# Rotating 96 images by 180 degrees: the innermost piece of the first group is turned ahead of the last quarter of the second group

## Chip, core and metric

The kernel runs on one core of a Trainium2 chip. The metric is the device time in microseconds (us) of one execution. Before the change its median over three runs is 121.98 us (121.88 to 122.0).

## The reference

The input is 32 x 3 images of 256 x 256 float32 numbers, 25.17 MB. Each image is rotated by half a turn:

```python
x = np.random.randn(32, 3, 256, 256).astype(np.float32)
out = np.rot90(x, k=2, axes=(-2, -1)).astype(np.float32)
```

Half a turn of a 256 x 256 image is the same as reversing its 65,536 numbers from end to end. Nothing is computed; 25.17 MB are read, reversed and written.

## The kernel before

The 96 images are taken in three groups of 32. In a group each image is cut into four quarters of E = 16,384 numbers, and each quarter lies in one of the 128 partitions of the on-chip memory. So a group is one tile of 128 x 16,384 float32 (8.39 MB), and the three groups have a tile each: A, Bt and Ct. A fourth tile, T (128 x 2,048), is scratch.

An image is reversed in two steps. VectorE reverses each partition's 16,384 numbers in place. The store then writes the four quarters of an image in reversed order (the `::-1` in `store`). VectorE's part is done by `swap(t, lo, w)`: it exchanges the w columns from lo on with the w columns that lie as far from the other end, both reversed, by three copies: T from the far piece, the far piece from the near one, the near one from T. `inside(t)` calls it four times, with pieces of J = 2,048 columns, from the two ends to the middle. The last of these, the innermost piece, is the middle of the tile.

All loads are issued at the start: the first 512 columns of A from ScalarE's queue, the rest of A, Bt and Ct, in that order, from SyncE's (SP's) queue. All stores go out on SP's queue too. SP runs through its DMA instructions in program order, and waits ahead of each store until the copies are done whose results the store reads. VectorE's copies keep program order as well (`keep_in_program_order`).

The order around the change is written by hand in lines 78 to 87. Three pieces of A are turned, and then a fourth that is cut: of its 2,048 columns the outer 896 (J - LAST) are turned at once, and the innermost 1,152 (LAST) only behind all of Bt. A's first 128 columns (LEAD) are stored as soon as the first swap has made them; the rest of A in one store, behind the innermost piece.

Each big DMA is split over 16 DMA engines, eight partitions each, and each partition is one packet of about 64 KB.

Of the kernel before, what the change touches and what calls it, by code (L numbers as in the profile page):

```python
# [2 lines left out]

os.environ.setdefault("NEURON_RT_ULTRASERVER_MODE", "4")

# [4 lines left out]


@with_exitstack
def kernel(
    ctx: ExitStack,
    tc: tile.TileContext,
    x: bass.AP,
    out: bass.AP,
):

    nc = tc.nc
    P = 128

    B, C, H, W = x.shape
    L = H * W
    G = 32
    E = L // 4
    J = E // 8

    x4 = x.rearrange("b c h w -> (b c) (h w)").rearrange(
        "(g n) (s e) -> g (n s) e", n=G, s=4)
    o4 = out.rearrange("b c h w -> (b c) (h w)").rearrange(
        "(g n) (s e) -> g n s e", n=G, s=4)  # L40

    pool = ctx.enter_context(tc.tile_pool(name="slots", bufs=1))
    A = pool.tile([P, E], x.dtype, tag="A")
    Bt = pool.tile([P, E], x.dtype, tag="B")
    Ct = pool.tile([P, E], x.dtype, tag="C")
    T = pool.tile([P, J], x.dtype, tag="T")

    def back(t, lo, hi):
        return t[:, hi - 1:(lo - 1 if lo else None):-1]

    def copy(dst, src):
        tc.keep_in_program_order(nc.vector.tensor_copy(out=dst, in_=src))  # L52

    def load(t, g, lo, hi, queue=nc.sync):
        return queue.dma_start(out=t[:, lo:hi], in_=x4[g][:, lo:hi])  # L55

    def store(t, g, lo, hi):
        return nc.sync.dma_start(
            out=o4[g][:, ::-1, lo:hi], in_=t[:, lo:hi])

    def swap(t, lo, w):
        hi = E - lo - w
        copy(T[:, 0:w], back(t, hi, hi + w))
        copy(t[:, hi:hi + w], back(t, lo, lo + w))
        copy(t[:, lo:lo + w], T[:, 0:w])

    def inside(t):
        for lo in range(0, E // 2, J):
            swap(t, lo, J)

    HEAD = 512
    load(A, 0, 0, HEAD, nc.scalar)
    load(A, 0, HEAD, E)
    load(Bt, 1, 0, E)
    load(Ct, 2, 0, E)
    LAST = 1152
    LEAD = 128
    for lo in range(0, E // 2 - J, J):
        swap(A, lo, J)
    swap(A, E // 2 - J, J - LAST)  # L80
    store(A, 0, 0, LEAD)
    inside(Bt)
    swap(A, E // 2 - LAST, LAST)
    store(A, 0, LEAD, E)
    store(Bt, 1, 0, E)
    inside(Ct)
    store(Ct, 2, 0, E)


# [1 line left out]
_INS = ['x']  # L91
_OUTS = [((32, 3, 256, 256), 'float32')]


# [23 lines left out]
```

## Time and profile before

| | |
|---|---|
| median of three runs | 121.98 us |
| the profiled execution | 122.03 us |
| its span, first to last instruction | 120.2 us |
| VectorE (DVE) busy | 44.6 us, 37% of the span |
| DMA queue q1 (SP), share of 16 engines | 96.7% |
| moved | 50.33 MB, 419 GB/s over the span |
| a copy of 128 x 2,048 | 1,227 ns |
| a copy of 128 x 1,152 | 760 ns |

Times in the views are microseconds from the start of the span. In the list of instructions a line gives the start, the duration, the engine, the source line and what is written from what; "SPq" is SP's queue issuing a DMA, not the transfer itself. The row "DMA" gives the busy share of the 16 DMA engines in equal slices of the stretch, in tenths, and "GB/s" what was moved; a packet's bytes are counted in the slice in which it starts. In the list of waits the numbers are the total, the number of waits, and the longest.

### The profile page before, as it was taken

The page shows a single profiled execution, that of the slowest core. Times are in us where ns is not written, and L with a number is a line of the kernel's source. Part 1 is how long each engine was busy: PE and PEld are TensorE (multiplying, and loading weights), DVE is VectorE, ACT ScalarE, POOL GpSimd, SP SyncE. Part 2 cuts the span into 40 slices and gives each one's busy share as a digit, 9 for nine tenths or more (in the row PEclk, how much of TensorE's full clock was granted, in tenths as well). Part 3 has the DMA queues.
Part 4 walks back from the last instruction along what each step waited for, and adds up shares of the span by engine and source line. Part 5 has one row for each costly group of instructions (what it writes and reads, how often), then busy time and mean ns, then how long its engine had stood idle before and what let it go on. Part 6 is the DMA issues. An engine that isn't in the chain of part 4 may idle for free.

```text
span 120.2 us, 98 instructions
## 1 busy us (share of the span) xinstructions
DVE 44.6 (37%) x39; POOL 0.2 (0%) x4
## 2 busy tenths in 40 slices
DVE  0000000499990099999759999400000000000000
POOL 0000000000000000000000000000000000000000
DMA  9888988899889988998889777988898889888980
GB/s 338 349 349 349 698 349 349 360 654 392 349 349 610 436 349 349 589 458 349 349 368 692 346 346 346 692 349 349 349 698 349 349 349 698 349 349 349 676 371 0
DMA packets 1152, 50.33 MB, mean 419 GB/s; under 512 B 128, under 2 KB 256, under 8 KB 384
## 3 DMA queue, kind: packets, MB, share of 16 engines
q1 hardware_dynamic: 1008, 50.07, 96.7%
q10 hardware_dynamic: 144, 0.26, 0.6%
HBM read 25.17 MB, written 25.17 MB: 419 GB/s over the span
## 4 chain that ended last, share of the span: by engine, by line
DMA 34%; DVE 27%; another core or an unknown queue 2%; issue 1%; SPq 0%; DVEq 0%
DMA Bt<-in_x_dram 34%; DVE T L52 9%; DVE Bt L52 8%; DVE Ct L52 8%; DVE A L52 1%; SPq L55 0%; DVEq L52 0%
## 5 line engine op out<-in xcount | busy, mean ns | idle before, releaser
L52 DVE COPY T<-A 128x2048 f32<-128x2048 f32 (+2 forms) x5 | 5.1, 1014 | 22.8 <-DMA A<-in_x_dram 22.7
L52 DVE COPY T<-Bt 128x2048 f32<-128x2048 f32 x4 | 4.9, 1227 | 6.2 <-DMA Bt<-in_x_dram 6.1
L52 DVE COPY T<-Ct 128x2048 f32<-128x2048 f32 x4 | 4.9, 1227 | 2.0 <-DMA Ct<-in_x_dram 1.9
L52 DVE COPY A<-T 128x2048 f32<-128x2048 f32 (+2 forms) x5 | 5.1, 1013 | 0.2
L52 DVE COPY A<-A 128x2048 f32<-128x2048 f32 (+2 forms) x5 | 5.1, 1013 | 0.2
L52 DVE COPY Bt<-T 128x2048 f32<-128x2048 f32 x4 | 4.9, 1227 | 0.1
L52 DVE COPY Ct<-T 128x2048 f32<-128x2048 f32 x4 | 4.9, 1227 | 0.1
L52 DVE COPY Bt<-Bt 128x2048 f32<-128x2048 f32 x4 | 4.9, 1226 | 0.1
L52 DVE COPY Ct<-Ct 128x2048 f32<-128x2048 f32 x4 | 4.9, 1226 | 0.1
L102 POOL MEMSET const-bfloat16-1.0<- 128x1 bf16 x1 | 0.1, 103 | 0.0
L102 POOL MEMSET const-uint8-127<- 128x1 uint8 x1 | 0.1, 103 | 0.0
L102 POOL MEMSET const-float32-1.0<- 128x1 f32 x1 | 0.1, 100 | 0.0
L102 POOL MEMSET const-float32-0.0<- 128x1 f32 x1 | 0.1, 99 | 0.2 <-issue 0.2
## 6 DMA issues: line engine op xcount, KB each, us to landing
out_dram<-A SPq DMA_DIRECT2D x1, 8128.0 KB, 21.2
A<-in_x_dram SPq DMA_DIRECT2D x1, 7936.0 KB, 21.9
A<-in_x_dram ACTq DMA_DIRECT2D x1, 256.0 KB, 22.1
out_dram<-A SPq DMA_DIRECT2D x1, 64.0 KB, 35.2
Bt<-in_x_dram SPq DMA_DIRECT2D x1, 40.8
Ct<-in_x_dram SPq DMA_DIRECT2D x1, 59.8
out_dram<-Bt SPq DMA_DIRECT2D x1, 39.9
out_dram<-Ct SPq DMA_DIRECT2D x1, 42.8
```

Source lines behind the costliest of these rows:

```text
L52: tc.keep_in_program_order(nc.vector.tensor_copy(out=dst, in_=src))
L102: nc = _bacc.Bacc("TRN2", target_bir_lowering=False, num_devices=1)
```

## The change

Two steps of VectorE change places. Bt's first three pieces are turned, then A's innermost 1,152 columns, then the big store of A is issued, and only then Bt's last piece is turned and Bt stored. The pieces, the copies and the transfers are the same.

```diff
     swap(A, E // 2 - J, J - LAST)
     store(A, 0, 0, LEAD)
-    inside(Bt)
+    for lo in range(0, E // 2 - J, J):
+        swap(Bt, lo, J)
     swap(A, E // 2 - LAST, LAST)
     store(A, 0, LEAD, E)
+    swap(Bt, E // 2 - J, J)
     store(Bt, 1, 0, E)
     inside(Ct)
     store(Ct, 2, 0, E)
```

## The prediction

> **What bounds the kernel now.** I read the page's DMA rows first, then what the SP queue waits for, then the order of work around the place that the change touches, and last the DMA starts in slices of 0.05 us there.
>
> ```profile
> span 120.2 us, 98 instructions
> DVE 44.6 (37%) x39; POOL 0.2 (0%) x4
> DMA  9888988899889988998889777988898889888980
> ...
> q1 hardware_dynamic: 1008, 50.07, 96.7%
> ```
>
> VectorE works 37% of the span; SP's DMA queue keeps the 16 DMA engines busy for 96.7% of it. So the chain of the DMA engines sets the end, and a copy matters only if a DMA engine runs dry for want of it. Each big DMA gives each engine eight packets of about 64 KB, one per partition; I call them rows. The trace's packet records chain into 48 big rows per engine: 24 of loads, 24 of stores. A load row of Bt or Ct takes 2.418 us (65,536 B, so 27.1 GB/s on one engine, 434 on sixteen) and the next starts as it ends.
>
> ```profile
> SPq L58 <- DVE A L52: 36.0, 2, 32.4
> SPq L58 <- DMA A<-in_x_dram: 20.8, 1, 20.8
> ...
> SPq L58 <- DVE Ct L52: 15.2, 1, 15.2
> ```
>
> SP sits 32.4 us between the first small store of A and the big one: the big store is held back for the last copy of A.
>
> ```profile
> 53.46 1.23 DVE L52 COPY T<-Bt 128x2048 f32<-128x2048 f32 x1
> 54.72 1.23 DVE L52 COPY Bt<-Bt 128x2048 f32<-128x2048 f32 x1
> 55.98 1.23 DVE L52 COPY Bt<-T 128x2048 f32<-128x2048 f32 x1
> 57.24 0.76 DVE L52 COPY T<-A 128x1152 f32<-128x1152 f32 x1
> 58.03 0.76 DVE L52 COPY A<-A 128x1152 f32<-128x1152 f32 x1
> 58.83 0.76 DVE L52 COPY A<-T 128x1152 f32<-128x1152 f32 x1
> 59.62 0.55 SPq L58 DMA_DIRECT2D out_dram<-A  x1
> 60.21 0.59 SPq L58 DMA_DIRECT2D out_dram<-Bt  x1
> 61.50 1.23 DVE L52 COPY T<-Ct 128x2048 f32<-128x2048 f32 x1 [1.92 <-DMA Ct<-in_x_dram]
> ```
>
> The first three lines are Bt's last quarter, the next three A's innermost piece: these six are exchanged. After them VectorE idles 1.92 us for the load of Ct.
>
> Now the seam between loads and stores, 60 to 62 us in 40 slices:
>
> ```profile
> GB/s 0 0 0 0 0 0 0 0 0 31 82 164 195 174 144 72 7875 3963 2703 82 2642 2632 20 20 20 1301 0 0 0 0 0 0 0 0 0 0 0 0 0 0
> ```
>
> Bytes are counted in the slice in which a packet starts. 7875 GB/s x 0.05 us is 394 KB: six rows of A (65,024 B each). So six rows start at 60.80 to 60.85, then three and two (eleven engines by 60.95), then two, two and one; the last starts at 61.25. The small numbers are the 512 B packets of the first store (LEAD), which has waited in the queue since 26.5. On the slowest engine they run right up to its first row (the three 20s ahead of 1301): eight packets, 0.19 us, and no idle time. The packet records say the same: its loads end at 61.06, its A row starts 0.197 us later. That engine also ends last, at 119.09 (the others at 118.81 to 118.94). Behind it come 1.16 us to the end of the span and 1.78 us outside it (execution 122.03, span 120.25). The eleven other engines end their loads at 60.45 to 60.70, are through LEAD 0.19 us later, and get A's rows only from 60.82 on. They idle up to 0.17 us. That is the only idle time there that the later release of A can explain.
>
> **The change, part by part.**
>
> VectorE: nothing is added. A's three copies of 0.76 us (2.28, with issue 2.38) move to 53.46-55.84; Bt's last three (3.68, with issue 3.78) move to 55.84-59.59. Sum 0. The work that follows on VectorE, Ct's turn, is released by a load at 61.4, 1.9 us later; if that cover were gone the cost would still be 0, as the order is exchanged and not lengthened.
>
> SP: the big store of A is issued at about 55.85 to 56.40 in place of 59.62 to 60.17. Bt's store still waits for VectorE at 59.6 and then goes out at once, 0.59 us earlier than now, since A's issue no longer stands before it; its rows are needed at 80, so this is worth 0. Behind it SP waits for Ct's last copy (76.6) as before; Ct's rows are needed at 99.4. No wait is added.
>
> DMA engines: issue start to first row is 60.82 - 59.62 = 1.20 us here. So A's rows lie ready from about 57.05, when each engine is in its second last load row (these start at 55.61 to 56.10), instead of 60.82. The eleven engines lose their wait of up to 0.17 us. The five others, the one that ends last among them, lose nothing that they have. So the first-order sum on the chain that sets the end is 0.
>
> The Trainium skill, page "DMA: Bandwidth & Descriptors", section "Specifications", puts the first byte on this path at about 0.6 us. By that A's rows would have been ready at 60.22 already, no engine would have waited, and the sum would also be 0; the row of 1.20 us decides.
>
> What the trace before does not show is a 64 KB store row waiting behind load rows. Bounds from its rows:
> - Gain: the slowest engine's last load row took 2.547 us, 0.129 over its usual 2.418, and the excess can only fall by 61.06, in the stretch in which eleven engines start A's rows together (their first rows too are long: 2.43 to 2.46 against 2.399 later). With A queued they start one by one as their loads end. If that burst made the excess, all 0.129 comes back: 121.85. More than this plus the 0.17 of idle time can't come from the seam.
> - Loss: load and store rows now run side by side from 60.65 (first loads' end plus LEAD) and not from 60.82, that is for 0.41 us ahead of 61.06 and not 0.24. At 0.129 per 0.24 us that is 0.22, so 0.09 more: 122.07.
>
> I take 0, between them: nothing says which of the two readings of that one long row holds. 121.98 - 0 = 121.98, own bounds 121.85 to 122.07; the profiled execution (122.03) stands 0.05 over the median.
>
> One rule speaks against the change. The same page, section "Two DMAs through the same engine are not ordered", says that an engine's read and write sides are separate queues and descriptors are pipelined. By that, a queued 64 KB store row could begin to be read while a load row is still being written, which LEAD, with 4 KB per engine, shows too little of. The row: with LEAD queued from 26.5 on, the load rows stay at 2.418 us, and with Bt's store queued behind A's, A's rows stay at 2.40. The sum by the rows is 0, by the rule's worst reading it is the second rival.
>
> **The rivals.**
>
> *The start at the seam gets cheaper (faster, over 0.2%).* It needs over 0.24 us: all of the 0.129 above, and besides an ordinary execution in which the slowest engine too waits for A, as the eleven did (up to 0.17). Together 0.30: 121.68. Against it: in the profiled execution that engine is 0.44 us (61.26 - 60.82) too late to wait at all. 12%.
>
> *Queued stores disturb the loads' end (slower).* The place: the last two load rows of the slowest engine, behind which A's rows now lie ready, and its first store row. Price: 0.129 for each of two rows gives 0.26 (122.24); the upper bound is the dearest start of a stage in this trace, where all engines begin their first row (2.897 us on the mean, against 2.342 for the next ones): 0.555, so 122.54. Middle 122.4. It decides when those two rows exceed 2.418 us by over 0.12 us each on the engine that ends last; on the others there is 0.15 us or more of slack. For it: the one row that did share the seam with store rows is the longest of the Bt and Ct load rows. Against: rows queued behind rows cost nothing anywhere else in this trace. It has no hard bound in the profile, as this pairing isn't shown. 36%.
>
> *The change doesn't do what it says:* SP issues in program order, and if the order were not kept, or A's rows came later than 60.8, time would be as now. This falls in with no change.
>
> **How the numbers follow.** No change to within 0.2% (0.24 us, about what a measurement of this kernel can tell): 52%, 121.98, its own range 121.85 to 122.10. Slower 36%, 122.24 to 122.54. Faster 12%, near 121.7. The range runs from 121.76, which takes in the gain bound with the spread of 0.1 of the three times, to 122.54, the upper end of the slower case; left out are most of the faster case and a tail of the slower.
>
> **What would show it.** Right: VectorE's copies of A at 53.5 to 55.8; the issue of A's store near 55.9 and of Bt's near 59.6; in the slices of the seam no block of six or more row starts in one slice, but starts spread from 60.6 to 61.3 as the loads end, the last near 61.2; last data at 119.0 to 119.1. Wrong on the slow side: row starts of the last two load rows drifting from 2.418 us apart, or A's last start beyond 61.4. Wrong on the fast side: the last start of A before 61.0, or the store rows under 2.399 us.

## The result and the profile after

The changed kernel takes 122.98 us (median of six runs, 122.72 to 123.51) against 121.99 us before (121.88 to 122.13): ratio 1.0083, 95% interval 1.0068 to 1.0098. It is slower by 1.0 us; the forecast was no change, and the range ended at 122.54. The profiled execution of the changed kernel is the slowest of its six, 123.51 us.

First the page's lines, then SP's wait ahead of the big store of A:

```profile
span 121.7 us, 99 instructions
DVE 44.6 (37%) x39; POOL 0.2 (0%) x4
DMA  9779977997799779878989878987998799879980
q1 hardware_dynamic: 1008, 50.07, 96.5%
```

```profile
SPq L58 <- DVE A L52: 32.2, 2, 28.7
```

VectorE's work is the same, the DMA engines are as busy as before (96.5%, before 96.7%), and SP waits 28.7 us instead of 32.4. Yet the span is 1.5 us longer: nothing in the shares tells where. The instructions around the seam:

```profile
53.62 0.76 DVE L52 COPY T<-A 128x1152 f32<-128x1152 f32 x1
54.42 0.76 DVE L52 COPY A<-A 128x1152 f32<-128x1152 f32 x1
55.21 0.76 DVE L52 COPY A<-T 128x1152 f32<-128x1152 f32 x1
56.00 0.55 SPq L58 DMA_DIRECT2D out_dram<-A  x1
...
59.78 0.54 SPq L58 DMA_DIRECT2D out_dram<-Bt  x1
63.03 1.23 DVE L52 COPY T<-Ct 128x2048 f32<-128x2048 f32 x1 [3.27 <-DMA Ct<-in_x_dram]
```

The order is the one forecast. The last line is not: Ct's load lands 1.5 us later than before, VectorE waits 3.27 us for it and not 1.92. So the time is lost ahead of the seam, in the loads. The DMA starts show the place: 57 to 65 us of the changed kernel, slices of 0.2 us (one row in a slice is about 328 GB/s):

```profile
GB/s 0 0 0 328 983 2949 328 328 328 0 0 0 0 0 0 0 0 0 0 0 0 0 31 1728 1096 1984 10 341 340 0 0 0 0 0 0 1626 975 1951 0 325
```

and the same stretch of the kernel before:

```profile
GB/s 0 0 0 0 0 2949 983 1311 0 0 0 0 0 0 0 0 0 69 146 3656 1329 330 0 0 0 0 0 0 0 0 0 3576 1300 325 0 0 0 0 0 0
```

Three clusters stand in each line: the last load rows, A's first rows, A's second rows. Before, the densest slices of the first two clusters lie 14 slices apart (58.0 and 60.8 us); after, 18 to 20 (58.0 and 61.6 to 62.0). From A's first to its second rows it is 12 slices in both. The packet records give the durations: the last load row takes 3.681 us on the mean of the 16 engines (2.432 before), the row ahead of it 2.424, every store row behind it 2.399 or 2.418, with no gap. One row per engine is 1.25 us longer on the mean. On the engine that ends last nothing of it comes back: it starts A's rows at 62.76 (before 61.26), and its data end at 120.57 (119.09). Its own last row took 3.885 us (2.547 before), which is 1.34 of these 1.50 us; the other 0.16 it was behind already when its load of A had ended, at 22.45 (22.29).

In what follows, "the last row" is that last load row, as a mean over the 16 engines of the profiled execution. "Growth" is its excess over 2.418 us. "Ready" is the start of the issue of A's big store plus 1.20 us, the interval that the prediction read off; 0.55 of it is the issue itself. The held store below shows it again (60.16 to 61.36); elsewhere it is an estimate from these two.

### The profile page after: what moved, and what is told of

Its sections match the earlier page's. It is cut to its first block, busy times and chain, and to the rows that moved or that the text cites. A ratio compares the mean times of both kernels' runs of the same rounds, so it can differ in the third digit from the quotient of the medians.

```text
span 121.7 us, 99 instructions
## 1 busy us (share of the span) xinstructions
DVE 44.6 (37%) x39; POOL 0.2 (0%) x4
## 2 busy tenths in 40 slices
DMA packets 1152, 50.33 MB, mean 413 GB/s; under 512 B 128, under 2 KB 256, under 8 KB 384
## 3 DMA queue, kind: packets, MB, share of 16 engines
q1 hardware_dynamic: 1008, 50.07, 96.5%
## 4 chain that ended last, share of the span: by engine, by line
DMA 34%; DVE 26%; another core or an unknown queue 3%; issue 1%; SPq 0%; DVEq 0%
DMA Bt<-in_x_dram 34%; DVE T L52 9%; DVE Ct L52 8%; DVE Bt L52 8%; DVE A L52 1%; SPq L55 0%; DVEq L52 0%
```

## The experiments

**Is it VectorE's order, or the queued store?** Three theories stood at first. Q: store rows that already lie in an engine's queue lengthen the load row ahead of them. V: VectorE's new order, with long copies beside the last row. I: the issue itself disturbs the rows under way. The first attempt to separate Q and V:

```diff
     swap(A, E // 2 - LAST, LAST)
-    store(A, 0, LEAD, E)
     swap(Bt, E // 2 - J, J)
+    store(A, 0, LEAD, E)
     store(Bt, 1, 0, E)
```

> VectorE's new order alone: A's innermost piece is turned ahead of Bt's last quarter as in the changed kernel, but A's big store is issued only behind Bt's last copy, near 59.6 us as in the kernel before. Theory Q (big store rows of A that already lie in an engine's queue lengthen the load row just ahead of them): the last load row stays near 2.43 us on the mean and the time at 122.0 (121.9 to 122.2). Theory V (VectorE's order: full 2,048-column copies beside the last load row slow it): the last load row stays near 3.7 us and the time near 123.0.

Measured 122.99 us, ratio 1.0087 (1.0072 to 1.0102), last row 3.505. By the expectation that would be V, but the list of instructions shows that the edit did nothing:

```profile
55.92 0.55 SPq L58 DMA_DIRECT2D out_dram<-A  x1
55.93 1.23 DVE L52 COPY T<-Bt 128x2048 f32<-128x2048 f32 x1
```

A's store went out at 55.92, ahead of Bt's last copies. Its line stands behind them, but SP waits only for the copies that the store reads. So this run is the changed kernel once more, and it decides nothing. The second attempt gives the store something to wait for:

```diff
-    swap(A, E // 2 - LAST, LAST)
-    store(A, 0, LEAD, E)
-    swap(Bt, E // 2 - J, J)
+    swap(A, E // 2 - LAST, LAST - 16)
+    swap(Bt, E // 2 - J, J)
+    swap(A, E // 2 - 16, 16)
+    store(A, 0, LEAD, E)
```

> VectorE's new order with A's big store held back in fact: all but the last 16 columns of A's innermost piece are turned ahead of Bt's last quarter, the last 16 behind it, so A's store can't be issued before about 59.9 us. Theory Q (store rows that lie in an engine's queue when its last load row begins, near 58.0 to 58.5 us, lengthen that row): no growth, last load row near 2.43 us, time 121.9 to 122.2. Theory V (VectorE's order): last load row 3.3 to 3.7 us, time near 123.0.

```profile
60.16 0.55 SPq L58 DMA_DIRECT2D out_dram<-A  x1
```

The last row took 2.419 us: VectorE's order costs nothing, V falls. The time was 122.57, ratio 1.0047 (1.0032 to 1.0062), above what was expected, for another reason. The three copies of 16 columns took 0.6 us, the issue came at 60.16 (before 59.62), and now all engines wait for A. The starts from 60 to 62 us in slices of 0.05 us:

```profile
GB/s 0 0 0 0 0 0 10 20 41 61 123 133 174 225 154 133 82 62 51 21 21 0 0 0 0 0 0 9103 6502 3901 1300 0 0 0 0 0 0 0 0 0
```

Seven rows of A start in one slice at 61.35 to 61.40, then five, three, one, after a pause in which nothing starts. The engine that ends last had its loads done at 60.86 and got A's row at 61.51. So there is also a price for being late.

**Does it matter how long the rows lie there?** A is turned whole ahead of Bt, and its store goes out at 38.52 us:

```diff
-    inside(Bt)
     swap(A, E // 2 - LAST, LAST)
     store(A, 0, LEAD, E)
+    inside(Bt)
     store(Bt, 1, 0, E)
```

> A is turned whole ahead of Bt and its big store issued near 38 us, some 23 us ahead of the loads' end. Theory Q: what counts is only that the rows lie there when the last load row is under way, so that one row grows to about 3.7 us, the others stay at 2.418, and the time is that of the changed kernel, 122.7 to 123.5. Theory I (the issue itself, the writing of the descriptors, disturbs the rows under way at that moment): rows near 38 to 40 us grow, the last load row stays at 2.43. Theory L (each load row with store rows queued behind pays): nine or more rows grow by 0.6 to 1.25 us each, time over 127.

```profile
38.52 0.55 SPq L58 DMA_DIRECT2D out_dram<-A  x1
```

122.9 us, ratio 1.0081 (1.0066 to 1.0096). The last row took 3.318 us; all other rows of Bt and Ct stayed at 2.418 to 2.421 on the mean, those near 38 to 40 us too. So neither the issue (I) nor the waiting along the way costs more than 0.003 us; only the load row that runs when the loads end pays, and once.

**When is the decision?** Three runs move only the moment of A's store, by the number of columns held back or by a part of Bt's last piece turned first. Its issue in the three, in the order in which they follow:

```profile
58.65 0.54 SPq L58 DMA_DIRECT2D out_dram<-A  x1
57.18 0.55 SPq L58 DMA_DIRECT2D out_dram<-A  x1
58.07 0.55 SPq L58 DMA_DIRECT2D out_dram<-A  x1
```

```diff
-    LAST = 1152
+    LAST = 512
```

> The kernel before with 512 in place of 1,152 columns held back, so A's big store is issued near 58.6 us in place of 59.6 and its rows should lie ready near 59.8, some 0.7 us ahead of the first engine's end of loads. Theory Q with a growing price: the last load row grows on all engines by 0.3 to 1.0 us, time 122.2 to 122.9. If the whole price is due as soon as the rows come while the last load row is under way: about 1.25 us, 123.0. If the rows must be there when that row starts: no growth, 122.0.

Issue at 58.65, ready near 59.85, 0.6 us ahead of the first engine's end of loads (60.42): last row 2.430, time 122.08, ratio 1.0009 (0.9999 to 1.0019). No price clear of the noise. The starts from 60 to 62 us:

```profile
GB/s 0 0 0 0 0 0 0 0 10 92 123 133 2745 4066 1444 1454 5325 1372 1352 1352 1321 20 1311 0 0 0 0 0 0 0 0 0 0 0 0 0 0 0 0 0
```

The rows begin spread out from 60.60 on, as the engines' loads end, the last in the slice from 61.10. Store rows of the early engines run beside load rows of the late ones here, and no load row is longer than 2.442.

```diff
-    swap(A, E // 2 - LAST, LAST)
-    store(A, 0, LEAD, E)
-    swap(Bt, E // 2 - J, J)
+    swap(Bt, E // 2 - J, 400)
+    swap(A, E // 2 - LAST, LAST)
+    store(A, 0, LEAD, E)
+    swap(Bt, E // 2 - J + 400, J - 400)
```

> The changed kernel with 400 columns of Bt's last quarter turned ahead of A's innermost piece, so A's store is issued near 57.1 us and its rows lie ready near 58.3, while the sixteen engines begin their last load rows (58.0 to 58.5). Theory Q with the decision at the start of the row: the engines split in two groups, those whose last load row begins after the rows came grow by 0.9 to 1.3 us, those that began before stay at 2.42; the time is set by the late ones, 122.5 to 123.1. If the price rises smoothly with the time that the rows lie there: all engines grow by a like amount, 0.5 to 1.0 us, time near 122.6. If only whole rows of waiting count: no growth, 122.0.

Issue at 57.18, ready near 58.4, while the last rows begin (57.98 to 58.64). All engines grew, to between 2.954 and 3.598, also those whose last row had begun before 58.4; mean 3.277, time 122.96, ratio 1.0073 (1.0056 to 1.0090). So the start of the row is not the point of decision; it lies later, inside the row.

```diff
-    LAST = 1152
+    LAST = 128
```

> The kernel before with 128 in place of 1,152 columns held back: A's big store is issued near 57.9 us, its rows should lie ready near 59.1, that is 1.4 to 1.9 us ahead of the engines' ends of loads (0.7 us more than with 512 held back, where nothing grew; 0.8 us less than the issue at 57.18, where the last load row grew by 0.86 us on the mean). Theory R (an engine reads ahead: once it has read its last load row, some way ahead of that row's end, it goes on to the packets queued behind it, and that delays the row's end): the price is between, 0.1 to 0.8 us of growth, uneven over the engines, those whose rows end last most; time 122.1 to 122.8. Theory S (what counts is whether the rows lie there when the row starts, with the issue at 57.18 just early enough): no growth, 122.0.

Issue at 58.07, ready near 59.3: six engines at 2.418 to 2.420, ten at 2.504 to 2.785, mean 2.565; time 122.13, ratio 1.0015 (1.0005 to 1.0025). The price falls from 0.86 to 0.15 to 0.01 us of growth as the rows come 2.3, 1.4 and 0.8 us ahead of the time at which a last row of 2.42 us would end on the mean (60.65). Theory S, with its decision at the start of the row, falls; R fits better: an engine goes on to what is queued some time before its last load row has ended. One part of R did not come: the rows that end last were to grow most, but the ten that grew began their row anywhere from 57.87 to 58.56, and the six that did not from 58.05 to 58.31. What picks the engines stays open.

**How far ahead does it reach?** The changed kernel, with each engine's loads ending in eight packets of 16 KB in place of two rows:

```diff
-    load(Ct, 2, 0, E)
+    load(Ct, 2, 0, 3 * E // 4)
+    load(Ct, 2, 3 * E // 4, E)
```

> The changed kernel with Ct's load cut in two, three quarters of the columns and then the last quarter, so that each engine ends its loads with eight packets of 16 KB (0.605 us each) in place of one of 64 KB every 2.418; A's rows lie ready from about 57.2, some 3.5 us ahead of the loads' end. Theory R: the delay falls on the last packet or two, together about 1 us as before, and the packets ahead of them stay at 0.605; time near 122.9. If every load packet with a store queued behind it pays: five or six packets grow, together well over 1 us. If the growth is a share of the packet just ahead of the store (1.1 of 2.42 us): 0.3 us, time near 122.3.

122.81 us, ratio 1.0074 (1.0059 to 1.0089). The eight packets took 0.611, 0.611, 0.612, 0.612, 0.613, 0.814, 1.118 and 0.695 us on the mean, though A's rows lay ready from about 57.2, when the third was under way. The last three lose 0.79 us together (0.20, 0.51, 0.08 over 0.611). Most of the loss is not on the packet next to the store but on the one before it. In stretches (start and end, length, VectorE, GpSimd, clock, DMA share, GB/s):

```profile
55.60:58.60 3.00, 2.90 (x4) 0.00 (x0) 1.00 1.00 426
58.60:61.60 3.00, 1.14 (x1) 0.00 (x0) 1.00 1.02 320
```

Full rate up to 58.6, then a quarter less, although the second stretch counts two of A's rows whole that begin in its last 0.12 us. The DMA share is 1.02, so the engines count as busy while they lose it.

**What is it in the queue that costs?** In all these runs the small LEAD store has lain behind the loads since 26.5, without a price. So either its size spares it, or A's big store is needed. The first small store is made wider, and A's big one stays near 59.6 to 59.8:

```diff
-    LEAD = 128
+    LEAD = 1024
```

> The kernel before with the first small store widened from 128 to 1,024 columns (packets of 4 KB in place of 512 B, 32 KB per engine, about 1.2 us of transfer), queued from 26.5 us on; A's big store still near 59.6 us. Theory Q by bytes queued behind the last load row: it grows by some 0.3 to 1.25 us, time 122.2 to 123.0. Theory Q only for big packets (64 KB): no growth, last load row near 2.42, A's rows start later by 1.0 us without idle time, time 121.9 to 122.1.

Last row 3.347, time 123.0, ratio 1.0087 (1.0071 to 1.0103): 32 KB per engine cost as much as all of A. The starts from 60 to 62 us in slices of 0.05 us; the first number that is not 0 is the first small packet, at the end of the first engine's loads (61.30 here, 60.45 in the kernel before):

```profile
GB/s 0 0 0 0 0 0 0 0 0 0 0 0 0 0 0 0 0 0 0 0 0 0 0 0 0 0 246 164 82 328 410 82 246 655 246 246 573 410 164 655
```

Half of that, LEAD = 512:

> The kernel before with a first small store of 512 columns: 8 packets of 2 KB, 16 KB per engine. If the price is that of reading the queued bytes ahead, up to some limit near 25 to 32 KB: the last load row grows by about half of what 1,024 columns cost, 0.4 to 0.6 us, time 122.4 to 122.6. If there is a threshold: either 0 (122.0) or 0.9 us (122.9).

```profile
GB/s 0 0 0 0 0 0 0 0 0 0 0 0 0 0 0 0 0 0 82 123 246 123 328 246 328 369 369 451 410 328 1720 1557 2867 5284 164 2703 2581 123 1352 1270
```

Last row 2.898, time 122.16, ratio 1.0015 (1.0003 to 1.0026). The first small packet starts at 60.90. The growth is half that of 1,024 columns, 0.48 against 0.93 us for 16 and 32 KB. It is not a threshold. The time grew by less than the row, by 0.18 us. The wider first store doesn't explain that: from the end of its loads to Bt's first row the engine that ends last takes 19.36 us with all three widths, so what the small store takes more the big one takes less. Why it grew by less stays open. And the same bytes in packets of 512 B, as several stores of 128 columns:

```diff
-    store(A, 0, 0, LEAD)
+    for lo in range(0, 8 * LEAD, LEAD):
+        store(A, 0, lo, lo + LEAD)
...
-    store(A, 0, LEAD, E)
+    store(A, 0, 8 * LEAD, E)
```

> The kernel before with eight small stores of 128 columns of A in place of one: per engine 64 packets of 512 B, 32 KB, the bytes of the store of 1,024 columns, queued from 26.5 us on; A's big store still near 59.6 us. If bytes behind the load row count: the last load row grows as with 1,024 columns, by 0.9 us, time near 122.9 and over, as the packets of 512 B cost 0.0235 us each (1.5 us for 64, 0.3 more than for the same bytes in big packets). If the size of the first packets counts: no growth, time near 122.3 by the dearer packets alone.

Last row 2.692; 123.73 us, ratio 1.0140 (1.0125 to 1.0155). The time says nothing on the question, because SP was held up, as its waits show:

```profile
SPq L58 <- DMA Ct<-in_x_dram: 19.0, 1, 19.0
```

SP waited for Ct's load before the eighth small store, so that one and A's big store went out only from 61.58 on, and A's first row started at 63.4. Seven small stores lay queued, 56 packets and 28 KB. With four (4 in place of 8 in the diff) SP isn't held:

> The kernel before with four small stores of 128 columns of A: per engine 32 packets of 512 B, 16 KB, against the 8 packets of 2 KB with 512 columns, where the last load row took 2.898 us on the mean; A's big store near 59.6 us as before. If bytes count: 2.9 us, and time near 122.2 to 122.5. If the number of packets read ahead is limited (7 x 8 packets of 512 B grew the row by only 0.27 us): 2.45 to 2.6 us, time 122.1 to 122.4.

Last row 2.747; 122.46 us, ratio 1.0045 (1.0030 to 1.0060). Packets of 512 B cost less than bytes alone would say: 0.33 us for 32 of them against 0.48 for 16 KB in packets of 2 KB, and 56 cost no more than 32 (0.27). The row fell in neither expected interval; bytes and the number of packets both seem to limit the price. In the runs with a wider LEAD, with four small stores and with the copy below, A's big rows lie ready too (near 60.7 to 61.0) before the lengthened last rows end on most engines, and no run takes them away at the same packet size. A share of theirs in these prices is not excluded; with seven small stores A's rows were not there, and the last row still grew by 0.27.

**Reading on-chip memory, or writing HBM?** A store does both. One DMA more copies 896 columns of A to a scratch tile S on the chip, queued near 26.5 ahead of LEAD:

```diff
+    S = pool.tile([P, 896], x.dtype, tag="S")
...
+    nc.sync.dma_start(out=S, in_=A[:, 0:896])
     store(A, 0, 0, LEAD)
```

> The kernel before with one DMA more, queued near 26.5 us ahead of the small store: 896 columns of A copied to a scratch tile on the chip, 8 packets of 3.5 KB per engine, 28 KB, read from on-chip memory but not written to HBM. They cost about 1.05 us of transfer by themselves. If it is the reading of on-chip memory ahead of time that lengthens the last load row: 3.2 us or so, as with 32 KB of store packets (3.347), time 123.5 to 123.9. If it is the writing to HBM: 2.42 to 2.45 us, time 122.8 to 123.1.

```profile
GB/s 0 0 0 0 0 0 0 0 0 0 0 0 0 0 0 0 0 0 0 0 0 0 0 0 0 0 0 72 0 215 215 359 287 215 574 287 287 645 358 358
```

Last row 3.337, time 123.9, ratio 1.0160 (1.0143 to 1.0177). The first packet behind the loads starts at 61.35. 28 KB per engine that never go to HBM lengthen the last load row as 32 KB of a store do. So it isn't the mix of HBM reads and writes. Loads queued behind loads cost nothing (2.418 throughout), and they too write on-chip memory; what the costly ones share in these runs is that they read it.

## Why the prediction was wrong

The mechanics of the edit were right. VectorE's sum was 0 and the copies stood where they were said to; SP issued A's store at 56.00 (said 55.85) and Bt's at 59.78 (said 59.6). The idle time of the eleven engines came back as said: all 16 now start A 0.197 us after their loads, their first rows take 2.399, and it is worth nothing by itself: with 512 columns held back every engine starts A 0.196 us after its loads too, and the time does not fall (1.0009). Ct's turn slid by 1.5 us and its store to 78.16, still 22 us ahead of its need.

The step that failed is the bounding of the operation that the trace did not show, a 64 KB store row queued behind a load row. Its value was taken as 0, its loss bound as 0.09. Behind it stands the opening premise that a copy matters only if a DMA engine runs dry for want of it; here no engine ran dry, and a copy that came earlier cost 1.0 us. The sign named for the slow side came: A's last start was to lie beyond 61.4, and it lay at 62.76. Over 2.418 us the last row grew by 1.26 us in the profiled execution, and by 0.86 to 1.09 in the three runs that followed with rows ready in time. Three pieces of that step were at fault:

- The loss bound was worked out from store rows *running* beside load rows of other engines. With 512 columns held back they run side by side and nothing grows. It is the engine's own queue that counts.
- The evidence against a loss was LEAD, which had waited 35 us without harm. LEAD is 4 KB per engine. The prediction said that this shows too little of the matter, and then took 0 all the same. Made 16 or 32 KB, LEAD costs 0.48 and 0.93 us of row; at the same rate of 0.03 us per KB, 4 KB would be 0.12, and the growth with it alone was 0.01. The nearest row of the trace was near in kind and far in size.
- Bt's rows behind A's were store behind store, and Ct's behind Bt's load behind load. The only seam between unlike kinds in the whole trace was the one in question.

The second rival had the sign and nearly the place: the last load row grew, though the one ahead of it did not (2.424) and A's first row became no longer (2.399). Its price of 0.26 to 0.55 stands against 1.0 us measured: it was built from the 0.129 us of one odd row and from a start of a stage that has nothing to do with it. It was given 36%, less than no change. That odd row of 2.547 was no lever either: with 512 columns held back the longest last row is 2.442, and the time does not fall (1.0009). What made it long stays open.

The section "Two DMAs through the same engine are not ordered" of the Trainium skill's page "DMA: Bandwidth & Descriptors", cited against the change, fits what was found: it says that read and write sides are separate queues, and here the last row pays 0.86 to 1.26 us for rows queued behind it. That an engine's read side goes on to on-chip reads while the last HBM data are still coming in, and that this delays them, is argued from the place (the last 2 us of the loads), from the bytes and from the on-chip copy; the inside of an engine is not in the trace. Why the time doesn't come back later, although data should then have been read ahead, stays open too: the 24 store rows of an engine take 57.88 us on the mean, before 58.03, which is 0.15 of 1.25.

So the kernel before sits in a window. A's rows ready about 0.8 us ahead of the loads' end cost nothing clear of the noise; 1.4 us ahead cost 0.15% in time, 2.3 us and more ahead 0.7 to 0.9%, and 0.54 us later than in the kernel before 0.47%. That the late edge lies where LEAD's 0.19 us are through is an estimate from that kernel, where A's rows come up to 0.17 us after them and cost nothing that a run shows. No version tried beats the kernel before.

## What to carry to other kernels

Where the DMA engines are the bound, look at the durations of single packets on either side of a change of direction: the busy share stays near full while a row takes half as long again. A store queued early behind loads on the same queue was not free here: have its rows arrive just as the loads end, and keep what fills the gap small. Before an unseen pairing is priced at 0, ask whether the row taken as evidence has the same size, not only the same kind; and before an edit is read as holding a DMA back, look in the list of instructions whether it was issued later.

## What the runs showed of the hardware that was not expected

- Packets that read on-chip memory, queued behind HBM loads on the same queue, lengthen the end of the loads: by 0.48 us for 16 KB per engine (0.33 in packets of 512 B), 0.92 for 28 KB of on-chip copy, 0.93 for 32 KB, 0.86 to 1.26 for the 508 KB of A; by 0.01 for 4 KB in packets of 512 B.
- Queued earlier, they cost no more (ready some 18 us ahead of the last rows: 0.90 us; ready about 1 us ahead of them: 1.09 and 1.26), and rows further ahead of the loads' end stay at 2.418 us.
- The loss falls on the last three of eight 16 KB packets (0.20, 0.51 and 0.08 us), most on the last but one, and not on the one next to the store.
